# Two transformer blocks on one core: the second block's attention and retention issue two heads' matmuls at a point, and its query and key transposes come eight at a time

## The chip, the core and the metric

The kernel runs on one NeuronCore of a Trainium2 chip. The core has engines that run side by side, each with its own list of instructions: TensorE (PE in the profile, with PEld for its weight loads), VectorE (DVE), ScalarE (ACT), GpSimd (POOL) and SyncE (SP, which here issues the loads from memory). They meet through counters (semaphores): an instruction can be made to wait until another engine's counter has reached a value. The metric is the device time of one execution in microseconds (us).

## The reference

Two blocks are applied to `x` of 256 tokens by 2048 columns, in float32. The change lies in the mixing part of the second block, which has eight heads of attention and eight heads of retention, each 128 wide. With 256 tokens there is one key block, so that the attention is plain causal attention inside it.

```python
h = rms_norm_2(x, g_mix[i])
z = h @ w_in[i]
aq, ak, av, rq, rk, rv, rg = jnp.split(z, split_at, axis=-1)
aq = rotate(rms_norm_2(aq, q_norm)); ak = rotate(rms_norm_2(ak, k_norm))
a_out = softmax(causal(aq @ ak.T / sqrt(128))) @ av          # per head
s = (rotate(rq) @ rotate(rk).T * 128 ** -0.5) * decay        # per head
r = s @ rv                                                   # per head
r = r * rsqrt(mean(r * r) + RMS_EPS) * g_ret
r_out = silu(rg) * r
x = x + concat([a_out, r_out]) @ w_o[i]
...
```

(The retention is written here in the form in which the kernel computes it, over all 256 tokens at once.) Behind it come a gated feed-forward part and a gated embedding part.

## The kernel before

Every large product streams its weights. A weight tile of 128 x 1024 float32 is loaded by SP into `raw`, split by ACT into a high part `wh` (L196) and by DVE into the rest `wl` (L207), and PE multiplies both with the activations into one of two `acc` accumulators. One such tile is a **slot**. `slot()` (which each product calls for each tile) writes, ahead of the tile's own matmuls, the high split of the tile four slots on (`HI`), the low split of the tile three slots on (`LO`) and the load of the tile seven slots on, and then calls `tick()`.

`tick()` is what places all smaller work. The evictions of finished chunks are generators in `self.ev` (the first two are stepped), and longer side work, such as attention, is a generator in `self.side` (the first is stepped). Whatever a generator writes up to its next `yield` goes into the engines' lists at that spot. On PE, such small work stands between two slots' bulk matmuls; such a spot is called a **point** below. There is no other scheduler: the order is that of the code, and the waits between engines are put in for every tile that one engine writes and another reads or reuses.

Small accumulators in PSUM are whole banks of 128 x 512 float32: `sc` (two buffers), `tr` (one) and `pv` (one).

- `ev_norm` (in `mix2`) evicts a chunk of queries or keys of the attention; at its end it transposes the four heads of 128 tokens into an `sc` bank (L1149), copies them to `aqk` by ACT (L1150), yields, and does so for the other 128 tokens.
- `att2` runs through steps `s` with two ticks each. A step first finishes what `late` holds (the softmax's division of the step before, L690 and L692, and the low part of the output, L717), then transposes the probabilities of head `s - 2` (`turn`: PE into `tr`, ACT copy to `aT`, L702), then computes the scores of head `s` into `sc` and their softmax (DVE maximum L678 and L683, two ACT exponentials L685), and then the values of head `s - 4` into `pv` (`values`), from where `hilo_plain` copies them by ACT to `aV` (L713) and rounds them into `y2a` (L714).
- `ret2` runs through steps `h` with one tick each: the values of head `h - 2` into one half of a `pv` bank, the scores of head `h` into `sc`, and DVE's multiplication with that head's `dk` table (L1300), which SP fetches one head ahead (L1287).

While `att2` runs, PE's bulk work is that of the retention's queries and keys (narrow tiles, 16 pairs of matmuls of 512 and 256 columns for two slots), and their eviction `ev_rope` gives DVE multiplications such as L1177.

Of the kernel before, what the change touches and what calls it, by code (L numbers as in the profile page):

```python
# [12 lines left out]
P = 128  # L13
T = 256
# [5 lines left out]
NEG = -1e30  # L20
# [95 lines left out]
class Net:  # L116
# [592 lines left out]

    def hilo_plain(self, R, j, src, key):  # L710
        nc = self.nc
        raw = self.t("dk", [P, 384], bufs=2, name="aV")[:, :T]
        nc.scalar.activation(raw, src, AF.Copy)  # L713
        nc.scalar.activation(R[:, j, 0, :], raw, AF.Copy)  # L714

        def rest():
            nc.vector.tensor_sub(R[:, j, 1, :], raw, R[:, j, 0, :].bitcast(F32))  # L717
            self.done.add((key, j))
        return rest
# [324 lines left out]
    def mix2(self):  # L1044
# [10 lines left out]
        mask = self.t("aB", [P, 2, T], bufs=2, name="cmask").rearrange("p a t -> p (a t)")[:, :T]  # L1055
# [44 lines left out]
        R1 = self.t("R1", [P, 2, 8, T], name="aqk")  # L1100
        R4 = self.t("R4", [P, 2, 8, T], name="rqk")
        rsq = self.t("rsq", [P, 2, 8])

        def ev_norm(c, which):
            def ev(acc):
                yield from self.wait("rs2")
                zs, sqs = [], []
                ss = self.t("rss", [P, 2, 4])
                zs, w = [], None
                for t in range(2):  # L1110
                    a4 = acc[:, t, :].rearrange("p (h d) -> p h d", h=4)
                    sq = self.t("tq", [P, 512], bufs=2)
                    sqs.append(sq)
                    nc.scalar.activation(sq, acc[:, t, :], AF.Square)
                    if t:
                        nc.vector.tensor_add(zs[0], zs[0], w)
                    z = self.t("ty", [P, 512], bufs=3).rearrange("p (h d) -> p h d", h=4)
                    w = self.t("ty", [P, 512], bufs=3).rearrange("p (h d) -> p h d", h=4)
                    zs.append(z)
                    cs = tabs[:, 2 * which, t, :].unsqueeze(1).broadcast_to([P, 4, P])  # L1120
                    nc.vector.tensor_mul(z, a4, cs)
                    for h in range(2):
                        a, b = slice(h * 64, h * 64 + 64), slice(64 - h * 64, 128 - h * 64)
                        sn = tabs[:, 2 * which + 1, t, a].unsqueeze(1).broadcast_to([P, 4, 64])
                        nc.vector.tensor_mul(w[:, :, a], a4[:, :, b], sn)
                    yield
                yield 1
                nc.vector.tensor_add(zs[1], zs[1], w)
                for t in range(2):
                    nc.vector.tensor_reduce(ss[:, t, :], sqs[t].rearrange("p (h d) -> p h d", h=4), mybir.AxisListType.X, ALU.add)  # L1130
                for t in range(2):
                    nc.vector.tensor_scalar(ss[:, t, :], ss[:, t, :], r2[:, t : t + 1], EPS, ALU.mult, ALU.add)
                yield
                rs = self.t("rsk", [P, 2, 4])
                flat = lambda a: a.rearrange("p a b -> p (a b)")
                self.rsqrt(flat(rs), flat(ss), 8)
                for t in range(2):
                    dst = rsq[:, t, 4 * c : 4 * c + 4] if which == 0 else rs[:, t, :]
                    nc.vector.tensor_scalar(dst, rs[:, t, :], sc["c"][:, t : t + 1], 128 ** -0.5 if which == 0 else 1.0, ALU.mult, ALU.mult)
                yield  # L1140
                for t in range(2):
                    if which:
                        nc.vector.tensor_mul(zs[t], zs[t], rs[:, t, :].unsqueeze(2).broadcast_to([P, 4, P]))
                yield
                yield
                for t in range(2):
                    pt = self.sc()
                    for h in range(4):
                        nc.tensor.transpose(pt[:, h * P : h * P + P], zs[t][:, h, :], self.ident)  # L1149
                    nc.scalar.activation(R1[:, which, 4 * c : 4 * c + 4, t * P : t * P + P],  # L1150
                                         pt.rearrange("p (h d) -> p h d", h=4), AF.Copy)
                    yield
            return ev

        def ev_a(dst, c0, key=None):
# [31 lines left out]
        av = self.t("S8a", [P, 2, 1024], name="av")  # L1187
        self.chunk("A", acts, ev_a(av, 0))
        self.chunk("A", acts, ev_a(av, 512, "av"))
        Y0 = self.region(0, "y2a")  # L1190
# [60 lines left out]

    def att2(self, R1, av, rsq, mask, Y0):
        Pm, PT, late = {}, {}, []
        for s in range(13):
            while late:
                late.pop(0)()
            if 2 <= s < 10:
                self.turn(s - 2, Pm, PT)
            if s < 8:
                q, k = R1[:, 0, s], R1[:, 1, s]  # L1260
                x = self.sc()
                self.mm(x[:, 0:128], q[:, 0:128], k[:, 0:128], True, True)
                self.mm(x[:, 128:384], q[:, 128:256], k[:, :], True, True)
                late.append(self.softmax(s, x, [mask[:, 128:256], mask], NEG, Pm,
                                         (rsq[:, 0, s : s + 1], rsq[:, 1, s : s + 1])))
            if 4 <= s < 12:
                h = s - 4
                o = self.pv()
                self.values(h, PT, av, o, slice(h * P, h * P + P))
                late.append(self.hilo_plain(Y0, h, o[:, :T], "z"))  # L1270
            yield
            yield

    def ret2(self, R4, rv, st):
        nc = self.nc
        o = self.t("S8a", [P, 2, 1024], name="ro")
        ss = self.t("gss2", [P, 16])
        rs = self.t("grs2", [P, 16])
        st["o"], st["rs"] = o, rs
        sT, po = {}, None  # L1280

        dks = {}

        def fetch(h):
            if h < 8:
                dks[h] = self.t("dk", [P, 384], bufs=2)
                nc.sync.dma_start(dks[h], self.ins["decay"][:, h, :])  # L1287

        fetch(0)
        yield from self.wait("rv")  # L1290

        def decayed(h):
            fetch(h + 1)
            dk = dks.pop(h)
            q, k = R4[:, 0, h], R4[:, 1, h]
            s = self.sc()
            self.mm(s[:, 0:256], k[:, 0:128], q[:, :], True, True)
            self.mm(s[:, 256:384], k[:, 128:256], q[:, 128:256], True, True)
            d = self.t("aP", [P, 384], bufs=4, name="sT")
            nc.vector.tensor_mul(d, s[:, :384], dk)  # L1300
            sT[h] = d

        for h in range(10):
            if h >= 2:
                g = h - 2
                d = sT.pop(g)
                hs = slice(g * P, g * P + P)
                if g % 2 == 0:
                    po = self.pv()
                b = (g % 2) * T  # L1310
                self.mm(po[:, b : b + P], d[:, 0:128], rv[:, 0, hs], True, True)
                self.mm(po[:, b + P : b + T], d[:, 128:256], rv[:, 0, hs], True, False)
                self.mm(po[:, b + P : b + T], d[:, 256:384], rv[:, 1, hs], False, True)
                if g % 2 == 1:
                    sq = self.t("tq", [P, 512], bufs=2)
                    nc.scalar.activation(sq, po, AF.Square)
                    nc.vector.tensor_reduce(ss[:, 2 * g - 2 : 2 * g + 2], sq.rearrange("p (h d) -> p h d", h=4), mybir.AxisListType.X, ALU.add)
                    for t in range(2):
                        nc.scalar.activation(o[:, t, (g - 1) * P : (g + 1) * P].rearrange("p (h d) -> p h d", h=2),
                                             po.rearrange("p (h t d) -> p h t d", h=2, t=2)[:, :, t, :], AF.Copy)  # L1320
                if g % 4 == 3:
                    m = self.t("nm", [P, 16], bufs=2)[:, :8]
                    nc.vector.tensor_scalar(m, ss[:, 2 * g - 6 : 2 * g + 2], 1.0 / P, EPS, ALU.mult, ALU.add)
                    self.rsqrt(rs[:, 2 * g - 6 : 2 * g + 2], m, 8)
                    self.done.add(("ro", g // 4))
            if h < 8:
                decayed(h)
            yield


def tables():
# [90 lines left out]
```

## Time and profile before

| what | value |
|---|---|
| time, median of 3 runs | 2473.68 us (2473.56 to 2474.97) |
| time of the profiled execution | 2474.46 us |
| its span, first to last instruction | 2472.7 us |
| TensorE busy (PE) | 2461.4 us, 100% of the span |
| VectorE busy (DVE) | 1667.5 us, 67% |
| ScalarE busy (ACT) | 1279.3 us, 52% |
| data moved, mean | 190 GB/s |

The span is what the profile can divide up; the 1.8 us around it lie outside the first and last instruction. A busy share is an average over the whole kernel, and matmuls are pipelined, so a share of 100% says that PE always had an instruction in it, and not that each was short.

### The profile page before, as it was taken

Reading aid. Unit: us, or ns where it says so; the run is one execution under the profiler, and the core shown is the slowest. Engines: PE = TensorE matmul, PEld = TensorE weight load, DVE = VectorE, ACT = ScalarE, POOL = GpSimd, SP = SyncE. Lnnn points to the kernel's source line nnn. Section 1 sums busy time; section 2 is a strip of 40 time slices with the busy share of each in tenths; the row PEclk is TensorE's granted clock in tenths of the full one; section 3 lists DMA queues with packets and bytes.
Section 4 is the critical chain, followed back from the end, with each engine's and each line's share of the span. In section 5 each row is a group of like instructions: output and inputs, shape, how many; then the busy total and the mean of one; then the engine's idle time right before and its main releaser. Section 6 shows DMA issues by size and latency. Waiting matters only on the chain.

```text
span 2472.7 us, 36486 instructions
## 1 busy us (share of the span) xinstructions
PE 2461.4 (100%) x14162; PEld 2152.6 (87%) x14162; DVE 1667.5 (67%) x2374; ACT 1279.3 (52%) x1713; POOL 8.4 (0%) x60
## 2 busy tenths in 40 slices
PE   9999999999999999999999999999999999999999
PEld 8888788888888888888888888888888888888888
DVE  6666667777755787767886765676666556666665
ACT  6545655665633565545644644555554434554453
POOL 0000000000000000000000000000000000000000
PEclk9999999999999999999999999999999999999999
DMA  7545455555555555555555455555555555555554
GB/s 246 189 145 192 158 188 190 194 196 192 192 195 195 191 193 196 196 199 191 198 179 187 162 183 190 182 194 190 196 194 191 195 196 192 192 196 198 192 201 148
DMA packets 133551, 469.30 MB, mean 190 GB/s; under 512 B 14961, under 2 KB 17393, under 8 KB 133377
## 3 DMA queue, kind: packets, MB, share of 16 engines
q1 hardware_dynamic: 133232, 466.95, 54.7%
q8 instruction: 111, 1.82, 0.3%
q14 instruction: 64, 0.52, 0.1%
q10 hardware_dynamic: 144, 0.01, 0.0%
HBM read 464.80 MB, written 2.10 MB: 189 GB/s over the span
## 4 chain that ended last, share of the span: by engine, by line
PE 99%; DMA 0%; DVE 0%; ACT 0%; issue 0%; SPq 0%; ACTq 0%
PE acc L262 95%; PE sc L262 2%; PE pv L262 1%; PE tr L700 0%; DMA raw<-weights 0%; PE sc L1149 0%; PE sc L1232 0%; PE sc L568 0%; ACT wh L196 0%; DVE ty L998 0%; DVE X L999 0%; PE tr L787 0%; SPq L430 0%; DVE ty L312 0%; DVE ty L977 0%
## 5 line engine op out<-in xcount | busy, mean ns | idle before, releaser
L207 DVE TENSOR_TENSOR wl<-raw,wh 128x1024 fp32r<-128x1024 f32 (+1 forms) x881 | 1068.9, 1214 | 757.4 <-PE acc L262 490.9
L196 ACT ACTIVATE wh<-raw 128x1024 fp32r<-128x1024 f32 (+1 forms) x881 | 925.1, 1051 | 842.2 <-PE acc L262 660.2
L262 PE MATMUL acc<-f,wh 128*128 128x512 f32 x2816 | 958.7, 389 | 0.0
L262 PE MATMUL acc<-f,wl 128*128 128x256 f32 x2816 | 777.4, 276 | 0.0
L262 PEld LDWEIGHTS acc<-f,wh 128*128 128x128 f32 x2816 | 528.5, 188 | 110.0
L262 PEld LDWEIGHTS acc<-f,wl 128*128 128x128 f32 x2816 | 528.5, 188 | 0.0
L262 PE MATMUL acc<-g,wh 128*128 128x512 f32 x1408 | 479.1, 389 | 0.0
L262 PE MATMUL acc<-g,wl 128*128 128x256 f32 x1408 | 388.7, 276 | 0.0
L262 PEld LDWEIGHTS acc<-g,wh 128*128 128x128 f32 x1408 | 264.3, 188 | 55.1
L262 PEld LDWEIGHTS acc<-g,wl 128*128 128x128 f32 x1408 | 264.3, 188 | 0.0
L262 PE MATMUL acc<-hp,wh 128*128 128x512 f32 x512 | 175.1, 390 | 0.0
L262 PE MATMUL acc<-hp,wl 128*128 128x256 f32 x512 | 141.4, 276 | 0.0
L262 PEld LDWEIGHTS acc<-hp,wh 128*128 128x128 f32 x512 | 96.1, 188 | 19.6
L262 PE MATMUL acc<-wh,m2b 128*128 128x512 f32 x320 | 102.7, 393 | 0.0
L262 PE MATMUL acc<-wh,m2a 128*128 128x512 f32 x320 | 102.2, 392 | 0.0
L262 PEld LDWEIGHTS acc<-hp,wl 128*128 128x128 f32 x512 | 96.1, 188 | 0.0
L899 ACT ACTIVATE ty<-tU,vec 128x256 f32<-128x256 f32 x88 | 48.2, 595 | 74.4 <-DVE tU L895 74.4
L310 ACT ACTIVATE tq<-acc 128x512 f32<-128x512 f32 x124 | 72.0, 580 | 4.7 <-PE acc L262 4.7
L262 PE MATMUL acc<-wh,h0a 128*128 128x512 f32 (+2 forms) x224 | 67.6, 379 | 5.1 <-ACT wh L196 5.1
L262 PEld LDWEIGHTS acc<-wh,m2a 128*128 128x128 f32 x320 | 60.1, 188 | 12.3
L262 PEld LDWEIGHTS acc<-wh,m2b 128*128 128x128 f32 x320 | 60.1, 188 | 12.2
L262 PE MATMUL acc<-h0a,wh 128*128 128x512 f32 x192 | 67.1, 394 | 0.0
(272 smaller groups left out, 2746.5 us busy)
## 6 DMA issues: line engine op xcount, KB each, us to landing
raw<-weights SPq DMA_DIRECT2D x863, 512.0 KB, 3.2
raw<-weights SPq DMA_DIRECT2D x10, 256.0 KB, 2.7
raw<-weights SPq DMA_DIRECT2D x8, 272.0 KB, 2.7
aB<-bias SPq DMA_DIRECT2D x8, 256.0 KB, 3.6
X<-xT SPq DMA_DIRECT2D x7, 256.0 KB, 6.4
dk<-decay SPq DMA_DIRECT2D x8, 192.0 KB, 3.9
out<-X SPq DMA_DIRECT2D x6, 256.0 KB, 2.6
pr<-pT SPq DMA_DIRECT2D x2, 256.0 KB, 4.6
```

The lines of the kernel that those rows point to most:

```text
L196: self.nc.scalar.activation(self.H[i][:, a], self.raw[i][:, a], AF.Copy)
L207: self.nc.vector.tensor_sub(self.L[i][:, a], r[:, a], self.H[i][:, a].bitcast(F32))
L262: self.nc.tensor.matmul(out, lhsT, rhs, start=start, stop=stop, skip_group_check=True, **kw)
L310: self.nc.scalar.activation(m, acc[:, :, T:], AF.Copy)
L899: nc.scalar.activation(y[:, b, :], u[:, b, 0:T], AF.Identity, scale=self.col("cw0", j), bias=self.col("b_ffn_conv", j))
```

## The change

Three things are regrouped; no product is added or left out.

- `ev_norm`: both halves of 128 tokens are transposed at one point, eight transposes into the two `sc` banks, with one `yield` behind both.
- `att2`: a step (now `g`, four ticks) takes two heads: one transposed head, the scores and softmaxes of two heads, the values of two heads into the two halves of one `pv` bank, and the other transposed head. The rest of the softmaxes and the low parts (`late`) come two ticks later.
- `ret2`: two heads a point, with two ticks between points. The tables `dk` get four buffers instead of two; four are fetched ahead of the loop, and each later one behind the multiplication that frees its buffer. (`aV` of `hilo_plain` shares these buffers.)

```diff
@@ hilo_plain
-        raw = self.t("dk", [P, 384], bufs=2, name="aV")[:, :T]
+        raw = self.t("dk", [P, 384], bufs=4, name="aV")[:, :T]
@@ ev_norm, behind the ACT copy of the transposes, in the loop over t
-                    yield
+                yield
@@ att2
         Pm, PT, late = {}, {}, []
-        for s in range(13):
+        for g in range(6):
+            if 1 <= g < 5:
+                self.turn(2 * g - 2, Pm, PT)
+            if g < 4:
+                for h in (2 * g, 2 * g + 1):
+                    q, k = R1[:, 0, h], R1[:, 1, h]
+                    x = self.sc()
+                    self.mm(x[:, 0:128], q[:, 0:128], k[:, 0:128], True, True)
+                    self.mm(x[:, 128:384], q[:, 128:256], k[:, :], True, True)
+                    late.append(self.softmax(h, x, [mask[:, 128:256], mask], NEG, Pm,
+                                             (rsq[:, 0, h : h + 1], rsq[:, 1, h : h + 1])))
+            if g >= 2:
+                o = self.pv()
+                for i in range(2):
+                    h = 2 * g - 4 + i
+                    self.values(h, PT, av, o[:, i * T : i * T + T], slice(h * P, h * P + P))
+                    late.append(self.hilo_plain(Y0, h, o[:, i * T : i * T + T], "z"))
+            if 1 <= g < 5:
+                self.turn(2 * g - 1, Pm, PT)
+            yield
+            yield
             while late:
                 late.pop(0)()
-            if 2 <= s < 10:
-                self.turn(s - 2, Pm, PT)
-            if s < 8:
...
-            if 4 <= s < 12:
-                h = s - 4
-                o = self.pv()
-                self.values(h, PT, av, o, slice(h * P, h * P + P))
-                late.append(self.hilo_plain(Y0, h, o[:, :T], "z"))
             yield
             yield
@@ ret2
-                dks[h] = self.t("dk", [P, 384], bufs=2)
+                dks[h] = self.t("dk", [P, 384], bufs=4)
...
-        fetch(0)
+        for h in range(4):
+            fetch(h)
         yield from self.wait("rv")
         def decayed(h):
-            fetch(h + 1)
...
             sT[h] = d
+            fetch(h + 4)
...
             if h < 8:
                 decayed(h)
-            yield
+            if h % 2:
+                yield
+                yield
```

How this moves the instructions is shown at three places. The first is PE's list at a point of the attention. Before, this is the point of step `s` = 6 (`tr` holds transposed probabilities, `sc` scores, `pv` values; the words in brackets name the engines whose counters an instruction waits for, ACT being called Activation):

```order
L700 MATMUL tr<-ident,aP 128x128 [waits DVE_49,Activation_49]
L700 MATMUL tr<-ident,aP 128x128 [waits DVE_49]
L700 MATMUL tr<-ident,aP 128x128
L262 MATMUL sc<-aqk 128x128
L262 MATMUL sc<-aqk 128x256
L262 MATMUL pv<-aT,av 128x256 [waits Activation_49]
L262 MATMUL pv<-aT,av 128x128
```

In the changed kernel, this is the point of `g` = 3, at the same slot:

```order
L700 MATMUL tr<-ident,aP 128x128 [waits DVE_49,Activation_49]
L700 MATMUL tr<-ident,aP 128x128 [waits DVE_49]
L700 MATMUL tr<-ident,aP 128x128
L262 MATMUL sc<-aqk 128x128
L262 MATMUL sc<-aqk 128x256
L262 MATMUL sc<-aqk 128x128
L262 MATMUL sc<-aqk 128x256
L262 MATMUL pv<-aT,av 128x256
L262 MATMUL pv<-aT,av 128x128
L262 MATMUL pv<-aT,av 128x256 [waits Activation_49]
L262 MATMUL pv<-aT,av 128x128
L700 MATMUL tr<-ident,aP 128x128 [waits DVE_49,PE_49]
```

The second head's matmuls have moved up into the point, and the second `pv` pair waits for ACT, while the first does not. (Two more `tr` rows follow.)

The second place is ACT's list around the same kind of point (`aT` is the copy of the transposed probabilities, `aP` the exponentials, `aV` the copy of the values out of `pv`). Before, at `s` = 6:

```order
L196 ACTIVATE wh<-raw 128x1024 [waits DMAHW2_49,PE_49]
L702 ACTIVATE aT<-tr 128x384 [waits PE_49]
L685 ACTIVATE aP,ast<-aP,ast,rsq 128x128 [waits DVE_49]
L685 ACTIVATE aP,ast<-aP,ast,rsq 128x256 [waits DVE_49]
L713 ACTIVATE aV<-pv 128x256 [waits PE_49]
L714 ACTIVATE y2a<-aV 128x256 [waits Activation_49]
```

In the changed kernel, at `g` = 3:

```order
L196 ACTIVATE wh<-raw 128x1024 [waits DMAHW2_49,PE_49]
L702 ACTIVATE aT<-tr 128x384 [waits PE_49]
L685 ACTIVATE aP,ast<-aP,ast,rsq 128x128 [waits DVE_49]
L685 ACTIVATE aP,ast<-aP,ast,rsq 128x256 [waits DVE_49]
L685 ACTIVATE aP,ast<-aP,ast,rsq 128x128 [waits DVE_49]
L685 ACTIVATE aP,ast<-aP,ast,rsq 128x256 [waits DVE_49]
L713 ACTIVATE aV<-pv 128x256 [waits PE_49]
L714 ACTIVATE y2a<-aV 128x256 [waits Activation_49]
L713 ACTIVATE aV<-pv 128x256 [waits PE_49]
L714 ACTIVATE y2a<-aV 128x256 [waits Activation_49]
L702 ACTIVATE aT<-tr 128x384 [waits PE_49]
```

Both heads' exponentials now stand ahead of the first head's `aV`, and both copies out of `pv` behind them.

The third place is PE's list at the point of `g` = 1 of the changed kernel, where two heads are transposed and scored and no values are due yet:

```order
L700 MATMUL tr<-ident,aP 128x128 [waits DVE_49] x2
L700 MATMUL tr<-ident,aP 128x128
L262 MATMUL sc<-aqk 128x128
L262 MATMUL sc<-aqk 128x256
L262 MATMUL sc<-aqk 128x128
L262 MATMUL sc<-aqk 128x256
L700 MATMUL tr<-ident,aP 128x128 [waits DVE_49,Activation_49]
```

Here the second head's transposes, which were two slots away before, have moved to the same point, and wait for ACT, which copies the one `tr` bank out.

## Rows read from the trace of the kernel before

**Rows 1.** The page's chain that ended last, shares of the span by engine.

```profile
PE 99%; DMA 0%; DVE 0%; ACT 0%; issue 0%; SPq 0%; ACTq 0%
```

**Rows 2.** Waits of PE: who waited for whom, total, times, longest (us).

```profile
PE acc L262 <- ACT wh L196: 5.1, 2, 4.6
```

**Rows 3.** Timeline of PE at a point (`s` = 6): start, length (us), instruction.

```profile
1405.71 0.49 PE L700 MATMUL tr<-ident,aP 128*128 128x128 f32 x3
1406.03 0.82 PE L262 MATMUL sc<-aqk 128*128 128x128 f32 x4
1406.69 0.81 PE L262 MATMUL pv<-aT,av 128*128 128x256 f32 x4
1407.26 0.48 PE L262 MATMUL acc<-m2b,wh 128*128 128x512 f32 x1
```

**Rows 4.** Timeline of ACT behind that point.

```profile
1405.79 1.06 ACT L196 ACTIVATE wh<-raw 128x1024 fp32r<-128x1024 f32 x1 [1.17 <-PE acc L262]
1406.75 0.47 ACT L702 ACTIVATE aT<-tr 128x384 f32<-128x384 f32 x1
1410.42 0.50 ACT L685 ACTIVATE aP<-aP,ast,rsq 128x128 f32<-128x128 f32 x1 [3.19 <-DVE ast L683]
...
1411.50 0.36 ACT L713 ACTIVATE aV<-pv 128x256 f32<-128x256 f32 x1
```

**Rows 5.** Timeline of DVE behind that point.

```profile
1407.22 1.39 DVE L1177 TENSOR_TENSOR ty<-w,tabR 64x512 f32<-64x512 f32 x2
1408.62 0.17 DVE L690 RECIPROCAL ast<-ast 128x2 f32<-128x2 f32 x1
...
1409.62 0.28 DVE L678 CUSTOM_DVE_ANT_0 aP<-sc,cmask 128x128 f32<-128x128 f32 x1
```

**Rows 6.** Timeline in `prep`, where one `pv` bank is filled twice: PE and ACT.

```profile
1256.60 0.61 PE L262 MATMUL pv<-ident,rf 128*128 128x128 f32 x4
...
1257.81 0.37 ACT L383 ACTIVATE rfb<-pv 128x256 f32<-128x256 f32 x1
...
1258.23 0.71 PE L262 MATMUL pv<-ident,rc 128*128 128x128 f32 x4 [1.02 <-ACT rfb L383]
```

**Rows 7.** Timeline of PE at the points `s` = 8 and `s` = 10.

```profile
1419.92 0.49 PE L700 MATMUL tr<-ident,aP 128*128 128x128 f32 x3
...
1432.94 0.81 PE L262 MATMUL pv<-aT,av 128*128 128x256 f32 x4
```

**Rows 8.** Timeline of ACT behind the points `s` = 8 and `s` = 10.

```profile
1421.34 0.38 ACT L713 ACTIVATE aV<-pv 128x256 f32<-128x256 f32 x1
...
1433.99 0.37 ACT L713 ACTIVATE aV<-pv 128x256 f32<-128x256 f32 x1
```

**Rows 9.** Timeline of PE around four transposes of `ev_norm`.

```profile
1269.45 0.39 PE L262 MATMUL acc<-wh,m2b 128*128 128x512 f32 x1
1269.68 0.60 PE L1149 MATMUL sc<-ident,ty 128*128 128x128 f32 x4
1270.03 0.48 PE L262 MATMUL acc<-wh,m2a 128*128 128x512 f32 x1
1270.35 0.40 PE L262 MATMUL acc<-wl,m2a 128*128 128x512 f32 x1
```

**Rows 10.** DMA issues: out<-in, count, KB each, median us to landing.

```profile
dk<-decay SPq DMA_DIRECT2D x8, 192.0 KB, 3.9
```

**Rows 11.** Busy time by stretch: PE, PEld, DVE, ACT, POOL, granted clock, DMA share.

```profile
1256.00:1260.00 4.00, 2.98 (x18) 2.46 (x17) 4.00 (x8) 1.72 (x3) 0.00 (x0) 1.00 0.50 154
...
2470.00:2472.70 2.70, 0.00 (x0) 0.00 (x0) 0.00 (x1) 0.00 (x0) 0.00 (x0) 0.76 0.29 97
```

**Rows 12.** Timeline of PE at the kernel's start.

```profile
4.59 0.80 PE L262 MATMUL acc<-wh,h0a 128*128 128x512 f32 x1 [4.59 <-ACT wh L196]
...
13.34 0.61 PE L262 MATMUL acc<-wl,h0a 128*128 128x512 f32 x1
13.77 0.42 PE L262 MATMUL acc<-wh,h0a 128*128 128x512 f32 x1
```

More of the change, by code (lines that the diff above doesn't have):

```diff
@@ L1253, in att2 @@
         Pm, PT, late = {}, {}, []
-        for s in range(13):
+        for g in range(6):
[19 more added lines that the diff above has]
+            yield
             while late:
                 late.pop(0)()
-            if 2 <= s < 10:
-                self.turn(s - 2, Pm, PT)
-            if s < 8:
[L1260 to L1265, printed above, removed]
-            if 4 <= s < 12:
-                h = s - 4
-                o = self.pv()
-                self.values(h, PT, av, o, slice(h * P, h * P + P))
-                late.append(self.hilo_plain(Y0, h, o[:, :T], "z"))
             yield
```

## The prediction

> **What bounds the kernel now.** I read the chain that ended last first: PE is 99% of it [rows 1], so time is won or lost only where PE's own list gets shorter or where PE stands still. The list of PE's waits is next: it has two entries, one at the kernel's start [rows 2] and one of 1.02 us, shown in its place [rows 6]. The second block's attention and retention therefore cost PE exactly the passes that they issue, and everything on DVE and ACT is hidden as long as nothing on PE waits for it. The third view is the timeline of the three engines at one attention point (step `s` = 6), which gives the pace at which DVE and ACT serve such a point [rows 3 to 5]. The reader is to see there that PE leaves the point 1.6 us after entering it (1405.71 to 1407.26 and a little), while ACT copies the values out of `pv` only at 1411.50, 5.8 us after the point began: before, nobody on PE asks for that copy until the next point.
>
> **What is removed.** Each point is a change of work for PE, and 15 of 30 go: four of the eight of the transposes, six of the twelve of the attention, five of the ten of the retention. One group of four transposes bounds what one costs [rows 9]. Bulk matmuls of 512 columns start 0.23 us apart (1269.45 to 1269.68). Four transposes take 0.35 (1269.68 to 1270.03), and the bulk matmul behind them holds 0.32 (to 1270.35), 0.09 more than normal. Four passes that start 0.11 apart (0.60 for the group less 0.27, about the length of one pass at this width, over three) are 0.44, which is just 0.35 and 0.09. So the change of work itself is near nothing; what may be left is a few hundredths for the slightly wider spacing behind a point. Bounds 0 and 0.09 a point; I take 0.05, since the visible 0.09 is accounted for by the passes: 15 x 0.05 = **0.75 us gained** (0 to 1.35).
>
> **What is added: a wait inside a point.** Before, a point holds one head's values, and the bank is copied out by ACT before the next point. Now two heads' values go into the two halves of one `pv` bank, and the order rows show that the second pair waits for ACT while the first does not. Two ACT instructions could be meant: the `aT` copy of the previous group, long done, or the first head's `aV` copy, which reads the half that has just been written. The rows of `g` = 1 and `g` = 3 decide it for me: the second `tr` of a point overwrites the bank that the point's own `aT` copy reads; at `g` = 1 it waits for ACT, at `g` = 3 it no longer does. Something ahead of it on PE must have waited for a later ACT instruction than that copy, and only the second `pv` pair can have. The same pattern is in this kernel already [rows 6]: one `pv` bank is filled, ACT copies the first half (1257.81, 0.37 long, ended 1258.18), and the second half's matmuls start at 1258.23, after 1.02 us of idle PE, 0.05 behind the copy. Bulk matmuls were waiting behind them and none was taken early.
>
> So at each of `g` = 2, 3, 4, 5 PE stands until the first head's `aV` is copied. What stands ahead of that copy on ACT decides the length.
>
> *g = 2 and 3* (scores and values). PE reaches the second pair after three transposes (0.32), two heads' scores (2 x 0.66) and one head's values (0.57 and 0.09 that overlap the next matmul, 0.66), all from the starts in rows 3: 2.30 us after the point begins. ACT must first do the exponentials of both heads. On DVE, `ty` ends 1408.61 [rows 5], 2.90 after the point's start; before, 1.0 us of `late` follows there, now the first softmax does at once. A softmax takes DVE 0.80 (from its start at 1409.62 to ACT's exponential at 1410.42, which waited for it) [rows 4, 5], so the heads' scales are ready at 3.70 and 4.50. A head's exponentials take ACT 1.08 (1410.42 to the start of `aV` at 1411.50): ACT is through with the first at 4.78 and with the second at 5.86. The copy adds 0.36 and the signal 0.05: PE goes on at 6.27. The wait is 6.27 - 2.30 = **3.97 us, twice**. Bounds: if DVE had nothing left of `ty` (1.39), 2.6; if it were still late by the 1.0 of `late`, 5.0.
>
> *g = 4* (transposes and values). The place is that of `s` = 8 [rows 7]. There `aV` ran from 1421.34 to 1421.72, directly behind `aT` [rows 8]; 1.80 and 0.05 behind the start at 1419.92, against an arrival at 0.32 + 0.66 = 0.98: **0.87 us**. *g = 5* (values only), the place of `s` = 10: `aV` ended 1434.36, 1.42 and 0.05 behind 1432.94, against 0.66: **0.81 us**. At both, what stands ahead is the split of a weight tile, so 0.4 (nothing ahead) to 1.4 (another half microsecond of ACT ahead) bound each.
>
> Sum: 2 x 3.97 + 0.87 + 0.81 = 9.62 lost, 0.75 gained: **8.9 us slower** (bounds 2 x 2.6 + 0.8 - 1.35 = 4.7 and 2 x 5.0 + 2.8 = 12.8).
>
> **Edits that I cost at nothing.** The second `tr` of a point must wait for the first's `aT` copy, since there is one such bank. At `g` = 1 PE comes to it after 0.32 + 2 x 0.66 = 1.64; the copy ends 1.51 after the point's start (1406.75 + 0.47) [rows 4]. The two heads' scores cover it; without that cover it would cost 1.2. At `g` = 2 to 4 the longer wait has already passed. Behind the exponentials on ACT stand the `wh` splits of coming tiles, up to 2 us late, but each is made four slots ahead, and PE's own standing still gives the time back. The eight transposes use both `sc` banks, which nobody else holds then. The `dk` tables come four at once, 576 KB ahead of the weights, 3.9 us to land [rows 10]; later fetches stand on SP's list behind DVE's multiplication, with the next weight load queued behind them, but that load reuses a `raw` buffer that DVE frees only after the same multiplication. The cover is the seven slots that loads are ahead; without it, one late tile would cost up to 3.9.
>
> **Rivals.** *(a) The clock falls in the long waits.* The granted clock is 1.00 in the stretch with PE's 1.02 us of idle, but 0.76 in the last 2.7 us, in which PE does nothing any more: part of it at the lower level, 1.2 GHz [rows 11]. The 3.9 us of idle at `g` = 2 and 3 are longer than that gap, and the rows don't say whether they are long enough. At the lower level a 512-column matmul takes 0.43 (13.34 to 13.77) [rows 12] and not 0.23. The only such stretch here, the start, held 18 matmuls from 4.59 to 13.77: 18 x 0.2 = 3.6 us. One fall would make it about 2484.5 to 2486, two up to 2490. The Trainium skill's "TensorE: Matmul & The Clock Gate", Part 1 (The HAM clock gate), says the same as a rule: an idle PE drops to half its clock and gets it back only by working. By that rule the two long waits would count more than their length; the trace shows the fall at its end, not after a gap of this size. Chance 0.17.
>
> *(b) No loss: the wait is for the older `aT` copy.* Then PE would not stand at `g` = 2 to 5 at all, and the time is the gain alone, 2473.68 - 0.75 = 2473, within 0.2%. For it: the name of the counter does not say which instruction. Against it: the missing wait at the second `tr`, and the wait that is there before [rows 6]. It decides at the end of the `aV` copy: if that lay before 2.3 us in the point, nothing would be lost. Chance 0.06; the middle ground, waits cut to under 5 us in all, is within it.
>
> *(c) More than the four waits.* ACT's late `wh` splits or the `dk` fetches reach PE as waits for weights. Against it: the lead of four slots, which took 14.2 us from the point of rows 3 to the first of rows 7 (1405.71 to 1419.92); for it: DVE and ACT work in bursts now. One tile late by 4 us gives 2487. Chance 0.06.
>
> **How the numbers follow.** The forecast, four waits and no fall of the clock, has a chance of 0.71. The profiled execution took 2474.46, its span of 2472.7 and 1.8 around it, 0.8 above the median of 2473.68. On its own time the sum gives 2483.4, on the median 2482.6; I name 2482.8. Its own range is 2479.5 to 2485.5. The range that leaves out 2 in 10 reaches up into (a) and (c) and not down to (b): 2479.5 to 2487.0. A difference of 0.2% (4.9 us) is about what can be told from no change here. Slower by more than that are the forecast, (a) and (c), less a small part for waits near their lower bounds: 0.92. Same: 0.07. Faster by more than 0.2% would need a gain of 5 us where the points bound it at 1.35: 0.01.
>
> **What would show it.** The list of PE's waits should have new entries of `pv` behind ACT `aV`, four in number, two near 4.0 and two near 0.8 us; PE's idle time in the attention should come to about 9.6 us, and ACT's `aV` should start behind four exponentials at `g` = 2 and 3. The transposes and the retention should show no wait, and save together under half a microsecond. The prediction is wrong if PE's wait names another instruction, if matmuls behind the long waits start 0.43 apart (then (a)), if PE waits for `wh` or `wl` in that stretch (then (c)), or if the second `tr` at `g` = 1 waits by a microsecond.

## The result, and the profile after

| | before | after |
|---|---|---|
| time, median (lowest to highest), us | 2474.31 (2473.45 to 2477.7, 6 runs) | 2488.22 (2485.14 to 2490.9, 6 runs) |
| profiled execution: time, span, us | 2474.46, 2472.7 | 2485.14, 2483.3 |
| median, after to before | | 1.0054, 95% interval 1.0043 to 1.0064 |

The changed kernel is slower by 13.9 us. The forecast was 2482.8 with a range to 2487.0; the median lies 1.2 us above that range. The profiled execution is the fastest of the six, so its rows show less than what the median run lost.

The list of PE's waits in the changed kernel (who waited for whom; total, times, longest in us), to be held against [rows 2]:

```profile
PE pv L262 <- ACT aV L713: 9.1, 4, 4.0
PE acc L262 <- ACT wh L196: 5.2, 2, 4.6
PE pv L262 <- ACT rfb L383: 1.0, 1, 1.0
```

The first entry is new and the other two are the old ones. Its four waits stand in the timeline of PE at the points `g` = 2 to 5 (start, length, instruction, in brackets the idle time ahead of it and who ended it), which answers to [rows 3, 7]:

```profile
1390.35 0.49 PE L700 MATMUL tr<-ident,aP 128*128 128x128 f32 x3
...
1391.99 0.82 PE L262 MATMUL pv<-aT,av 128*128 128x256 f32 x4
1396.64 0.92 PE L262 MATMUL pv<-aT,av 128*128 128x256 f32 x4 [3.83 <-ACT aV L713]
...
1398.77 0.39 PE L262 MATMUL acc<-m2b,wh 128*128 128x512 f32 x1
...
1408.63 0.49 PE L700 MATMUL tr<-ident,aP 128*128 128x128 f32 x3
1408.96 1.48 PE L262 MATMUL sc<-aqk 128*128 128x128 f32 x8
1410.27 0.82 PE L262 MATMUL pv<-aT,av 128*128 128x256 f32 x4
1415.06 1.52 PE L262 MATMUL pv<-aT,av 128*128 128x256 f32 x4 [3.97 <-ACT aV L713]
1416.37 0.85 PE L700 MATMUL tr<-ident,aP 128*128 128x128 f32 x3
1416.87 0.78 PE L262 MATMUL acc<-m2b,wh 128*128 128x512 f32 x1
1417.44 0.41 PE L262 MATMUL acc<-m2b,wl 128*128 128x256 f32 x1
1417.65 0.63 PE L262 MATMUL acc<-m2b,wh 128*128 128x512 f32 x1
1418.08 0.41 PE L262 MATMUL acc<-m2b,wl 128*128 128x256 f32 x1
1418.30 0.56 PE L262 MATMUL acc<-m2b,wh 128*128 128x512 f32 x1
1418.69 0.28 PE L262 MATMUL acc<-m2b,wl 128*128 128x256 f32 x1
1418.81 0.40 PE L262 MATMUL acc<-m2b,wh 128*128 128x512 f32 x1
...
1429.01 0.82 PE L262 MATMUL pv<-aT,av 128*128 128x256 f32 x4
1430.53 0.92 PE L262 MATMUL pv<-aT,av 128*128 128x256 f32 x4 [0.70 <-ACT aV L713]
...
1442.82 0.81 PE L262 MATMUL pv<-aT,av 128*128 128x256 f32 x4
1444.28 0.92 PE L262 MATMUL pv<-aT,av 128*128 128x256 f32 x4 [0.65 <-ACT aV L713]
```

The reader is to see two things at `g` = 3. The second head's values stand for 3.97 us although the first head's went out at once; and behind that wait everything is stretched: the pass of 512 columns at 1416.87 lasts 0.78, where the pass at that place lasts 0.48 in [rows 3], and the next two last 0.63 and 0.56, where 0.40 is normal; the start of the next pass lies 0.43 behind that of the one at 1417.65, which is the pace of the kernel's start [rows 12]. ACT's timeline at the same point shows why the copy comes so late (compare [rows 4]):

```profile
1409.68 0.47 ACT L702 ACTIVATE aT<-tr 128x384 f32<-128x384 f32 x1
1412.51 0.49 ACT L685 ACTIVATE aP<-aP,ast,rsq 128x128 f32<-128x128 f32 x1 [2.36 <-DVE ast L683]
...
1414.64 0.36 ACT L713 ACTIVATE aV<-pv 128x256 f32<-128x256 f32 x1
```

`aT` is done at 1410.15. `aV` starts behind both heads' exponentials and ends at 1415.00, and PE goes on 0.06 later. The windows of the same kernel (busy time of PE, PEld, DVE, ACT, POOL, then the granted clock, as in [rows 11]) tell the stretching apart from the waiting:

```profile
1390.00:1398.00 8.00, 4.17 (x28) 3.68 (x27) 4.73 (x16) 4.74 (x13) 0.00 (x0) 1.00 0.36 131
...
1413.00:1418.00 5.00, 2.94 (x10) 2.66 (x11) 0.39 (x4) 3.60 (x12) 0.00 (x0) 0.72 0.00 1
```

At `g` = 2 PE waits 3.83 us and the clock stays at 2.4 GHz; at `g` = 3 it waits 3.97 and part of the stretch is at 1.2 GHz. In this execution, then, the clock fell behind one of two waits of nearly equal length. What that cost can be read from the starts: the passes from PE's resumption to the fourth `wh` pass take 3.75 us at `g` = 3 (1415.06 to 1418.81) and 2.13 at `g` = 2 (1396.64 to 1398.77), so 1.6 us were lost beyond the wait.

### The profile page after: what moved, and what is told of

The parts are those of the page before. It is cut to its first block, busy times and chain, and to the rows that moved or that the text cites. A ratio compares the mean times of both kernels' runs of the same rounds, so it can differ in the third digit from the quotient of the medians.

```text
span 2483.3 us, 36487 instructions
## 1 busy us (share of the span) xinstructions
PE 2462.8 (99%) x14162; PEld 2153.5 (87%) x14162; DVE 1667.2 (67%) x2374; ACT 1280.3 (52%) x1713; POOL 8.4 (0%) x60
## 4 chain that ended last, share of the span: by engine, by line
PE 98%; DVE 1%; ACT 0%; DMA 0%; issue 0%; SPq 0%; DVEq 0%; ACTq 0%
PE acc L262 95%; PE sc L262 2%; PE pv L262 1%; PE tr L700 0%; DMA raw<-weights 0%; ACT aP L685 0%; ACT wh L196 0%; DVE wl L207 0%; PE sc L1149 0%; DVE ty L1177 0%; PE sc L1232 0%; PE sc L568 0%; DVE ty L998 0%; DVE aP L678 0%; ACT aV L713 0%
```

## The experiments

Four kernels ran on one chip beside a median of 2473.92 for the kernel before, three on another beside 2474.8. Differences below are to the one beside them, unless said otherwise.

**Copies behind both values.** The changed kernel, with ACT's two copies emitted behind both heads' values:

```
                 for i in range(2):
                     h = 2 * g - 4 + i
                     self.values(h, PT, av, o[:, i * T : i * T + T], slice(h * P, h * P + P))
+                for i in range(2):
+                    h = 2 * g - 4 + i
                     late.append(self.hilo_plain(Y0, h, o[:, i * T : i * T + T], "z"))
```

> The changed kernel with both heads' values issued before either head's copy out of the bank; the grouping into points is untouched. Theory 1 (PE's four waits for the first head's copy, and the lower clock that follows the two long ones, are the whole loss): the four entries of PE behind the copy vanish, the granted clock stays at 1.000 until PE has finished, and the time is 2473.0, between 2472.3 and 2474.5, 0.3 to 1 us below the kernel before or level with it. Theory 2 (the grouping itself costs, by bursts on VectorE and ScalarE and late weight tiles): more than 3 us of the loss stay, 2477 or more.

Measured: 2472.89 us (2472.28 to 2473.5), ratio 0.9996 (0.9987 to 1.0005). The timeline of PE at `g` = 2 of this kernel:

```profile
1390.18 0.49 PE L700 MATMUL tr<-ident,aP 128*128 128x128 f32 x3
1390.51 1.48 PE L262 MATMUL sc<-aqk 128*128 128x128 f32 x8
1391.82 1.47 PE L262 MATMUL pv<-aT,av 128*128 128x256 f32 x8
1393.12 0.49 PE L700 MATMUL tr<-ident,aP 128*128 128x128 f32 x3
```

All eight passes into `pv` go in one piece, and the list of PE's waits has no entry for `aV`. The whole loss hangs on the order of two copies: the grouping of heads, the bursts on DVE and ACT and the merged transposes are still there and cost nothing that can be told from this ratio, whose interval reaches from 3.2 us gained to 1.2 lost.

**Attention as before, and attention alone.** The first takes the function `att2` of before into the changed kernel and leaves the other edits (shown); the second is its reverse and puts the changed `att2`, and the four `dk` buffers that it needs, into the kernel before:

```
-        for g in range(6):
-            if 1 <= g < 5:
...
+        for s in range(13):
```

> The attention as in the kernel before; the transposes by eight, the retention by two heads and the four tables ahead as in the changed kernel. Theory 1: these parts gain what their points cost, 9 x 0.05 = 0.45 us by the forecast, so 2473.3 (2472.5 to 2474.3), and no wait of PE beyond those of the kernel before. Theory 2: the retention's tables, four at once, or its bursts cost 1 us or more: 2475 or above.

> Only the attention by two heads (and the four buffers of the table, which its copies share). Theory 1: the whole loss is here: four waits of 9.1 us in all and the lower clock behind the long ones, 2484 to 2491, a median near 2488, like the changed kernel within 1 us. Theory 2: about half of it, below 2483, the rest coming with the other two edits.

Measured: without the attention's edit 2473.39 us, ratio 0.9998 (0.9989 to 1.0007), with no wait of PE beyond those of the kernel before; with it alone 2487.26 us, ratio 1.0057 (1.0045 to 1.0070), the changed kernel's own. The profiled execution of the attention alone took 2489.51 and has the same list entry as after, 9.1 us in four waits. Its windows show where most of the 4.4 us arise by which it is longer than the profiled execution of after:

```profile
1396.50:1404.00 7.50, 6.18 (x22) 5.43 (x23) 0.00 (x0) 2.86 (x9) 0.00 (x0) 0.54 0.00 0
...
1417.00:1424.00 7.00, 5.12 (x17) 4.47 (x18) 0.22 (x2) 3.42 (x11) 0.00 (x0) 0.51 0.00 1
```

Here the clock fell at both long waits, of 3.83 and 3.96 us, and stayed low for longer. By the starts of the same passes, as above, 2.6 us were lost behind the first wait (1397.82 to 1403.61, 5.79 us, where `g` = 2 of the changed kernel takes 3.15) and 2.4 behind the second (1418.88 to 1424.06, 5.18 against 2.81). Two waits of nearly the same length thus cost 1.6 us beyond it in one execution and 5.0 in another. The other 1.0 us of the 4.4 comes from elsewhere: the point `g` = 2 begins 1.2 us later here (1391.54 against 1390.35).

**Values first.** Both heads' values go ahead of the scores in a point, with the copies as in the changed kernel:

```
+            if g >= 2:
+                o = self.pv()
+                for i in range(2):
...
             if g < 4:
                 for h in (2 * g, 2 * g + 1):
...
-            if g >= 2:
-                o = self.pv()
-                for i in range(2):
```

> The changed kernel with the values of two heads ahead of the scores of two heads inside a point, so that the first head's copy stands ahead of the exponentials on ScalarE. All four waits stay, each as short as the two short ones were (0.8 to 0.95 us). Theory 1 with the clock: short waits don't lower the clock, so 2473.6 + 4 x 0.87 - 0.7 = 2476.4 (2475.5 to 2477.5) and a granted clock of 1.000 up to PE's end in every run, and runs that agree within 1 us. If the extra loss beyond the waits came from something else than long idle stretches (the bank filled twice, the second transposes in a point): it stays at 3 to 5 us, 2480 or more.

Measured: 2477.19 us (2476.68 to 2481.03), ratio 1.0014 (1.0006 to 1.0023). The waits in the profiled execution:

```profile
PE pv L262 <- ACT aV L713: 2.8, 4, 0.7
```

The copy now stands behind no exponentials, so all four waits are short ones, of about 0.7 us, and the clock did not fall in this execution. Of the 3.3 us that remain over the kernel before, 2.8 are these; the other half a microsecond is about what this list leaves out, 0.16 us a wait (see the sizes of the waits below). The runs spread over 4.4 us and not over the 1 us expected, above all by the one at 2481.03, which the last section takes up.

**The wait kept, with passes in it.** This and the next two dose the clock:

```
                     late.append(self.hilo_plain(Y0, h, o[:, i * T : i * T + T], "z"))
+                    if i == 0 and g < 4:
+                        t = self.tr()
+                        for n in range(27):
+                            nc.tensor.transpose(t[:, n % 3 * P : n % 3 * P + P], self.ident, self.ident)
```

> The changed kernel with 27 transposes of the identity behind the first head's values at the two points that wait long (g=2 and g=3). Their results are read by nobody; each takes about 0.11 us by the 14 passes of a point in 1.9 us, so some 3.0 us of passes stand inside a wait of 3.97 us, and ScalarE's copy comes no earlier. Theory 1 (what the changed kernel loses beyond its four waits is TensorE at 1.2 GHz behind the two long idle stretches): the second head's values start at the same place of their point, about 6.3 us after its begin, the wait in the list of waits is 1.0 us at each of the two, no stretch at 1.2 GHz stands between the start and TensorE's end, and the time is that of the waits alone, 2483.2 us (2482.3 to 2484.3), against 2488.2 of the changed kernel; the runs lie closer together than its 5.8 us. Theory 2 (the residue has nothing to do with the idling: the order of the two heads' groups itself or the copies cost it): as the changed kernel, 2486 to 2490.

Measured: 2483.32 us (2482.63 to 2483.87), ratio 1.0036 (1.0023 to 1.0048). The timeline of PE at `g` = 2:

```profile
1390.39 0.49 PE L700 MATMUL tr<-ident,aP 128*128 128x128 f32 x3
...
1392.68 3.11 PE L1275 MATMUL tr<-ident 128*128 128x128 f32 x27
1396.68 0.92 PE L262 MATMUL pv<-aT,av 128*128 128x256 f32 x4 [0.89 <-ACT aV L713]
```

and the windows of both points:

```profile
1390.00:1398.00 8.00, 7.11 (x55) 6.58 (x53) 4.76 (x16) 4.72 (x13) 0.00 (x0) 1.00 0.42 131
1408.00:1418.00 10.00, 8.99 (x66) 8.24 (x65) 5.31 (x17) 5.53 (x15) 0.00 (x0) 1.00 0.32 105
```

The second head's values start 6.29 us behind the point's begin, exactly as in the changed kernel (1390.35 to 1396.64), so the delay is untouched; only PE is busy for 3.11 us of it. (The expected 0.11 us a pass holds, though 1.9 us over 14 passes, some of them of 256 columns, would be 0.14.) The clock is 1.00 throughout, the runs lie within 1.2 us of each other, and the time is 4.9 us less than the changed kernel's (5.4 by the distances to the kernel before on either chip); the highest of these runs lies 1.3 us below the lowest of the changed kernel's. Useless work in the wait made the kernel faster: these 5 us belong to the idling, not to the delay.

**The wait made longer.** The first head's values are copied seven times over at the two long points:

```
+        for n in range(7 if key == "z" and j in (0, 2) else 1):
+            nc.scalar.activation(raw, src, AF.Copy)
-        nc.scalar.activation(raw, src, AF.Copy)
```

> The changed kernel with ScalarE's copy of the first head's values made seven times in place of once at the two long points: 6 more of about 0.3 us ahead of the second head's values, so the two waits become some 1.8 us longer, about 5.7 us. Theory 1: the waits add 3.6 us, and each is followed by a stretch at 1.2 GHz as long as in the slowest runs or longer, so it comes out above the sum: 2492 us (2489.5 to 2497). Theory 2: the changed kernel's time and 3.6 us, 2491.8 (2490.5 to 2493); the test is the granted clock behind the waits.

Measured: 2491.93 us (2491.88 to 2493.02), ratio 1.0072 (1.0059 to 1.0085). The list of waits (the copy is L714 in this kernel), then PE's timeline at `g` = 2 and the windows behind both points:

```profile
PE pv L262 <- ACT aV L714: 14.0, 4, 6.3
```

```profile
1399.08 1.65 PE L262 MATMUL pv<-aT,av 128*128 128x256 f32 x4 [6.33 <-ACT aV L714]
...
1403.09 0.63 PE L262 MATMUL acc<-m2b,wh 128*128 128x512 f32 x1
...
1404.10 0.40 PE L262 MATMUL acc<-m2b,wh 128*128 128x512 f32 x1
```

```profile
1396.50:1404.00 7.50, 4.92 (x17) 4.31 (x18) 0.00 (x0) 3.93 (x11) 0.00 (x0) 0.54 0.00 0
...
1420.50:1428.00 7.50, 5.67 (x20) 4.96 (x21) 0.00 (x0) 3.24 (x9) 0.00 (x0) 0.54 0.00 0
```

The waits grew by 2.4 each and not by 1.8, since a copy that repeats takes 0.4. The median fits, but the account under it is another than the one expected: against the kernel with passes in the wait, 8.6 us, the longer waits are 14.0 - 9.1 = 4.9 and the clock is 3.7; between the two profiled executions (2493.02 and 2483.51) it is 4.6. PE's rows give 4.7 in the profiled one: 2.2 behind the first wait (1399.08 to 1404.10, 5.02 us for passes that take 2.81 at `g` = 2 of the changed kernel) and 2.5 behind the second. The changed kernel's median had 4.9 for the clock, so the longer waits did not make it dearer. A granted clock of 0.54 over 7.5 us leaves 0.6 us at the upper level, and PE resumed only 2.6 us into the first of the windows: the clock was low for some 2 us while PE still stood, and that part of the low stretch cost nothing. In these runs a longer wait made the fall surer and not dearer: all five have a mean granted clock of 0.997, and they lie within 1.2 us of each other, where the changed kernel's have 0.997 to 0.999 and spread by 5.8. The median could not have told the two theories apart, since both named about 2492; the granted clock does.

**The wait made shorter.** The first head's values go between the two heads' scores, so that the copy stands behind two exponentials (the `pv` tile is then taken ahead of the loop):

```
             for i in range(2):
                 if g < 4:
                     h = 2 * g + i
...
                 if g >= 2:
                     h = 2 * g - 4 + i
                     self.values(h, PT, av, o[:, i * T : i * T + T], slice(h * P, h * P + P))
```

> The changed kernel with the first head's values between the two heads' scores in each point: ScalarE's copy of them stands behind two exponentials in place of four, and TensorE has the second head's scores to do in the meantime. The copy comes about 1.1 us earlier, and the second head's values wait some 2.7 us in place of 3.9 us at g=2 and g=3, and 0.9 us at g=4 and g=5 as before. Without a lower clock that gives 2483.3 - 2.2 = 2481.1 us (2480.0 to 2482.0). Theory 1 holds either way: where the granted clock stays at 2.4 GHz behind such a wait the runs lie within 1.5 us of each other there, where it falls they lie up to 4 us higher and apart. Theory 2: 2488.2 - 2.2 = 2486 (2484.5 to 2487.5) without a stretch at 1.2 GHz.

Measured: 2482.89 us (2481.02 to 2487.2), ratio 1.0038 (1.0024 to 1.0052). PE's timeline at the two points, and the windows behind them:

```profile
1395.44 1.04 PE L262 MATMUL pv<-aT,av 128*128 128x256 f32 x4 [2.77 <-ACT aV L713]
...
1414.42 0.92 PE L262 MATMUL pv<-aT,av 128*128 128x256 f32 x4 [2.91 <-ACT aV L713]
```

```profile
1395.44:1396.20 0.76, 0.76 (x4) 0.71 (x5) 0.00 (x0) 0.76 (x3) 0.00 (x0) 0.94 0.00 0
1396.00:1400.00 4.00, 4.00 (x17) 3.56 (x16) 0.00 (x0) 1.97 (x7) 0.00 (x0) 0.57 0.00 0
1400.00:1420.00 20.00, 17.09 (x104) 14.94 (x103) 13.09 (x31) 10.14 (x20) 0.00 (x0) 1.00 0.33 106
```

The waits are 1.1 us shorter, as expected, and the lowest run, 2481.02, lies where 2481.1 was expected without a fall (whether it had none, no trace shows). The median lies below the 2484.5 to 2487.5 of theory 2. The clock still falls, in the profiled execution behind the shorter of the two waits and not behind the longer one; the runs spread over 6.2 us, more than the 4 us named.

## Why the prediction was right, and where it was wrong

**The bound and the place: right.** PE is 98% of the chain, against 99% in [rows 1]. The wait is the one named: the second head's `pv` matmuls stand for ACT's `aV` copy of the first head, which reads the other half of the bank, as in [rows 6]. The Trainium skill's "PSUM — Partial Sum Buffer", section "PSUM bank collisions raise a hardware error", asks that semaphores keep engines apart by bank and quadrant of the partitions, and not by address. The program's waits do that here, as the 3.97 us in which PE waits for a copy of columns that it does not write agree; no run shows what would happen without them.

**The sizes of the waits: right.** The forecast counted a wait from the moment at which PE could have started the second head's values, 0.66 behind the start of the first's. On that measure the rows give 3.99 (1391.99 to 1396.64, less 0.66), 4.13, 0.86 and 0.80 for 3.97 twice, 0.87 and 0.81; in sum 9.78 for 9.62. The list's 9.1 is smaller since it counts from the end of the first values (0.82 long), 0.16 later at each wait.

**The points' gain: in keeping, not shown.** With the wait taken away the kernel is 1.0 us below the one before, where 0.75 was named; the interval of that ratio reaches from a gain of 3.2 us to a loss of 1.2.

**The edits at no cost: right.** The second `tr` at `g` = 1 does not wait:

```profile
1377.45 0.49 PE L700 MATMUL tr<-ident,aP 128*128 128x128 f32 x3
1377.77 1.48 PE L262 MATMUL sc<-aqk 128*128 128x128 f32 x8
1379.09 0.53 PE L700 MATMUL tr<-ident,aP 128*128 128x128 f32 x3
```

The `dk` tables take 4.5 us to land in place of 3.9 [rows 10] and no weight is late behind them: rival (c) has no row in the list of waits. Rival (b), no loss, is ruled out by the same list. All other edits together, without the attention's, leave the time where it was.

**The clock: the step that failed.** The forecast's sum put work at half rate behind the two long waits at nothing; measured, it is 4.9 us (5.4 by the distances to the kernel before). 2482.8 is the time of four waits and no fall, and the kernel with passes in its waits gives just that: 2483.32, which is 8.5 above the kernel beside it, for 8.9. What the sum lacks is rival (a), which the prediction had at about the right price (2484.5 to 2486 for one fall, up to 2490 for two; the runs lie at 2485.14 to 2490.9) and gave a chance of 0.17. That price was read from the pace of the start alone: the profile gives the start a granted clock of 1.00. The changed kernel's rows have the same 0.43 where its granted clock fell. The reason given was that the rows don't say whether 3.9 us of idle PE is long enough. With nothing to decide it, that was no ground for so low a chance, and the upper end of the range was set between one fall and two. The runs show that 3.8 to 4.0 us is often long enough: in the two profiled executions with such waits the clock fell at three of four, with 6.3 us at two of two, with 2.8 and 2.9 at one of two, and with 1.0 us or less at none. That this is what parts 2483 from 2488 is shown by the passes put into the wait. The mean granted clock of the changed kernel's six runs goes the same way: 0.999 at 2485.14, 0.998 at 2487.60 and 2487.66, 0.997 at 2488.77, 2489.63 and 2490.9. Which of these had one fall and which two, no trace shows, except for the first.

## What to carry to other kernels

When two results share one PSUM bank and the program's waits go by the bank, as here, issue all matmuls into it before the first copy out of it; otherwise the second result waits for whatever stands ahead of that copy on its engine, here four exponentials and 4 us. (A second `pv` bank, which would part the two results, was not tried.) On a kernel that TensorE bounds, price a stall like those here, of 2.8 to 6.3 us, at its length and, where the clock falls, a further 1.6 to 2.6 us for work at half rate behind it, and reckon with a spread from run to run, since equal stalls are not always followed by a fall. If such a stall can't be avoided, passes that keep TensorE busy in it may give the second part back, as the 27 transposes did here.

## What the runs showed of the hardware

The low clock follows PE's idling, but when it begins is not tied to PE's resumption. With waits of 6.3 us it was at 1.2 GHz some 2 us ahead of the first resumption and 1.2 us or more ahead of the second; behind the wait of 2.77 us the granted clock was still 0.94 over the first 0.76 us of resumed work, and 0.57 over the stretch behind it (1396 to 1400). So what a fall costs is half of the low stretch that has work in it. The Trainium skill's "TensorE: Matmul & The Clock Gate", section "HAM oscillation — how this bites in real kernels", reckons the penalty as half of the whole throttled time. By that rule the stretch of 7.5 us at 0.54 in the kernel with longer waits would cost about 3.5 us; PE's rows there, from 1399.08 to 1404.10, make it 2.2, and where they differ the rows decide.

One thing stays open. The profiled execution of the kernel with the values first took 2481.03 us, 2.8 us more than any other of its eleven runs. No wait beyond the four and no fall of the clock accounts for it. In a stretch of its second block PE's pairs of passes start 0.35 us apart,

```profile
1593.55 0.40 PE L262 MATMUL acc<-y2b,wh 128*128 128x512 f32 x1
...
1593.90 0.40 PE L262 MATMUL acc<-y2b,wh 128*128 128x512 f32 x1
```

where the kernel with the copies behind has them 0.34 apart:

```profile
1587.43 0.39 PE L262 MATMUL acc<-y2b,wh 128*128 128x512 f32 x1
...
1587.77 0.39 PE L262 MATMUL acc<-y2b,wh 128*128 128x512 f32 x1
```

The granted clock is 1.00 in both. Some 270 pairs in a row, from 1571 to 1665, have this slower pace, and 270 x 0.01 = 2.7 us is the size of the excess. Shorter stretches of it stand in other traces too, such as 30 pairs of the changed kernel from 1432 to 1442, also at a granted clock of 1.00. Why the passes come 3% slower there was not found.
